# Three quarters of a down projection as seven block products: a hybrid trunk layer on one core

## The chip, the core and the metric

The kernel runs on one core of a Trainium2 chip. The core has five engines that run side by side: PE (TensorE, the matmuls), DVE (VectorE), ACT (ScalarE), POOL (GpSimd) and SP (SyncE, which issues loads). POOL and ACT issue transfers too; all go over the core's 16 DMA engines. The metric is the time of one execution on the device in microseconds (us), and less is better.

## The reference, cut to what matters

One layer: a token mixer, then the part that the change touches, a squared-ReLU MLP on 1024 frames of 1024 channels with a hidden width of 4096, and a last norm.

```
u2 = rms_norm(x, ln2) * (1.0 + scale2) + shift2
hid = jnp.square(jax.nn.relu(u2 @ w_up))      # 1024 -> 4096
x = x + gate2 * (hid @ w_down)                # 4096 -> 1024
return rms_norm(x, final_norm)
```

All is fp32.

## The kernel before

Activations lie transposed, channels on the 128 partitions and frames along the row, in tiles of 1024 frames or halves of 512. A matmul takes a 128x128 piece of a weight and 512 frames and sums into one of four banks ("mm"). To keep fp32 accuracy with the faster fp32r matmul, each operand is split: the high part is a rounding copy (ACT, whi or the first half of a hid tile), the low part what is left (DVE, wlo). A product is then three matmuls: high by high, high by low, low by high. Weight tiles (whi, wlo) have four buffers each, raw weights (wraw) three.

*Up projection.* The first four hidden tiles are plain products. The other 28 are computed in pairs by strassen_pair (L136): the weights of two column tiles, in two halves of the 1024 input channels, and the input in two halves of channels and two of frames make a 2x2 by 2x2 block product. It needs seven block products instead of eight, each of 12 matmuls (4 k x 3), with sums of weight blocks made on DVE (s12, s34), ready sums of input blocks (X), and sums of results on DVE (cu, cq, cy). up_evac squares the ReLU on ACT into hid, and POOL stores the tile to hid_d in device memory.

*Down projection* (L868). The 4096 hidden channels go in 8 blocks b of four tiles. For each, four tiles come back from hid_d through hr (POOL's queue, two buffers) and are split, hida or hid. Then for each of 8 output tiles f the plain product proj runs: 4 k x 3 x 2 halves = 24 matmuls into two banks, and DVE adds the result times gate2 into the residual y (in the code x1, loaded on SP at b = 0). The last block goes in three parts of frames (PARTS), so that the last norm overlaps with it. The first two tiles of every other block (hida) lie in the pool of hr, which exists during the up projection; the others lie in memory that the up projection's operands hold until its end.

A scheduler puts the instructions of each engine in order when the program is built; at run time each engine works strictly in that order, and each instruction waits for the data and the buffers it needs.

Of the kernel before, what the change touches and what calls it, by code (L numbers as in the profile page):

```python
# [7 lines left out]
F32 = mybir.dt.float32  # L8
# [29 lines left out]
def hybrid_trunk(tc, xT, par, hrows, crow, wada1, wada2, win, wdt, wco, wso, wo, wup, wdn, out):  # L38
# [42 lines left out]
    hid_d = dp.tile([32, P, T], F32, name="hid_d")  # L81
# [54 lines left out]
    def strassen_pair(tp_, w0, w1, X, evac):  # L136
# [29 lines left out]
        cu, cq, cy = [tp_.tile([P, H], F32, name=n) for n in ("cu", "cq", "cy")]  # L166
# [11 lines left out]
        prod(c, w34, 1, X["22"], False, True)  # L178
        tt(cy, c, cu, ALU.add)
# [638 lines left out]
    ws = [load_w(wup[i]) for i in range(4)]  # L818
# [21 lines left out]
    ph = tc.alloc_tile_pool(name="hids", bufs=2, side="right", reuse_waits="tile")  # L840
    pe_ = tc.alloc_tile_pool(name="up", bufs=2, side="right", reuse_waits="tile")
    def load_hid(i):
        hr = ph.tile([P, T], F32, name="hr")
        pool.dma_start(hr, hid_d[i])
        return hr

    for f in range(4, 32, 2):
        hid = [pe_.tile([P, T], F32, name="hid", bufs=3) for _ in (0, 1)]

        def up_evac(i, h, src):  # L850
            r = hid[i][:, hs[h]]
            act.activation(r, src, AF.Relu)
            act.activation(r, r, AF.Square)

        strassen_pair(pe_, wup[f], wup[f + 1], X, up_evac)
        for i in (0, 1):
            st_ = pool.dma_start(hid_d[f + i], hid[i])
        if f == 24:
            with tc.issue_after(st_.ins):
                hrs = [load_hid(i) for i in range(2)]  # L860
# [4 lines left out]
    p7 = tc.alloc_tile_pool(name="p7", bufs=2, reuse_waits="tile")  # L865
    xp = tc.alloc_tile_pool(name="x2", bufs=1, reuse_waits="tile")
    x1 = [[xp.tile([P, H], F32, name=f"y{f}{h}") for h in (0, 1)] for f in range(8)]
    for b in range(8):  # L868
        hid = []
        for i in range(4):  # L870
            hr = hrs.pop(0) if hrs else load_hid(4 * b + i)
            if i < 2 and b % 2 == 0:
                t = ph.tile([P, 2, T], F32R, name="hida")
            else:
                t = p7.tile([P, 2, T], F32R, name="hid", bufs=6)
            split(t[:, 0, :], t[:, 1, :], hr)
            hid.append(t)
        hh = [[t[:, 0, hs[0]], t[:, 0, hs[1]]] for t in hid]
# [103 lines left out]
```

## Time and profile before

| | before |
|---|---|
| time, median of 3 runs (lowest to highest) | 2155.35 us (2151.59 to 2156.64) |
| the profiled execution, its own time | 2155.5 us |
| span of its instructions | 2153.7 us |
| busy: PE, DVE, ACT, POOL | 98%, 65%, 40%, 5% |
| up projection's pairs | about 1520 to 1786 us |
| down projection with the last norm | 1786 to 2154 us |

The span is the time from the first to the last instruction in the trace; the time of an execution has a little around it. A busy share is a mean over the span; what an engine costs is read stage by stage.

### The profile page before, as it was taken

The numbers are of one execution on the slowest core, as the hardware profiler recorded it, in microseconds if no ns is written. First come the engines' busy times: TensorE is split into PE (matmuls) and PEld (weight loads), VectorE is DVE, ScalarE is ACT, GpSimd is POOL, SyncE is SP. The second block draws the span as 40 slices with busy tenths as digits, with TensorE's granted clock in tenths as the row PEclk, the third lists the DMA queues.
The fourth block names the chain that finished last, engine by engine and source line by source line (L and its number), as shares of the span: only waits on it lengthen the run. The fifth ranks groups of instructions, "written<-read, shape, count | busy, mean of one in ns | idle before, by whom it ended". The sixth has DMA issues, their size and how long they took to land.

```text
span 2153.7 us, 26047 instructions
## 1 busy us (share of the span) xinstructions
PE 2119.8 (98%) x9920; PEld 1731.3 (80%) x9920; DVE 1399.0 (65%) x2144; ACT 870.0 (40%) x1436; POOL 109.0 (5%) x200
## 2 busy tenths in 40 slices
PE   7999999999999999999999999999999999999998
PEld 4778878888888788888878888888888888888887
DVE  7876787765786767666885658756755555444444
ACT  4433333224565636455663321334544453211212
POOL 0000000000000000000000000021000000000003
PEclk8999999999999999999999999999999999999999
DMA  8226554123233223233356676532233346322212
GB/s 299 77 99 204 198 176 166 64 76 125 52 101 115 82 95 101 74 109 87 100 164 248 232 256 214 195 132 93 101 106 116 117 147 231 120 88 89 89 40 79
DMA packets 115472, 283.27 MB, mean 132 GB/s; under 512 B 10466, under 2 KB 45666, under 8 KB 115347
## 3 DMA queue, kind: packets, MB, share of 16 engines
q1 hardware_dynamic: 86882, 187.02, 27.0%
q0 software_dynamic: 16192, 58.73, 7.9%
q10 hardware_dynamic: 12272, 35.85, 4.2%
q8 instruction: 78, 1.28, 0.2%
q14 instruction: 48, 0.39, 0.1%
HBM read 218.45 MB, written 63.11 MB: 131 GB/s over the span
## 4 chain that ended last, share of the span: by engine, by line
PE 87%; issue 6%; DVE 3%; DMA 2%; ACT 1%; POOL 1%; SPq 0%; DVEq 0%; POOLq 0%; ACTq 0%
PE mm L145 21%; PE mm L111 19%; PE mm L114 19%; PE mm L112 19%; PE B L600 2%; PE B L605 2%; PE C L622 1%; DMA wv<-in_wada 1%; DVE wada L291 1%; PE A L577 1%; DMA x<-in_xT 1%; POOL wv L415 1%; DVE ul L46 1%; DVE x L46 0%; PE A L578 0%
## 5 line engine op out<-in xcount | busy, mean ns | idle before, releaser
L111 PE MATMUL mm<-uh,whi 128*128 128x512 f32 x768 | 303.0, 398 | 3.7 <-ACT uh L104 3.2
L112 PE MATMUL mm<-ul,whi 128*128 128x512 f32 x768 | 304.7, 397 | 0.0
L94 ACT CAST whi<-wraw 128x1024 fp32r<-128x1024 f32 x125 | 131.4, 1051 | 425.8 <-PE mm L112 403.7
L145 PE MATMUL mm<-t,whi 128*128 128x512 f32 x944 | 290.5, 390 | 2.8 <-DVE cq L43 2.8
L114 PE MATMUL mm<-uh,wlo 128*128 128x512 f32 x768 | 246.6, 396 | 1.9 <-DVE wlo L43 1.9
L43 DVE TENSOR_TENSOR wlo<-wraw,whi 128x1024 fp32r<-128x1024 f32 (+1 forms) x191 | 215.8, 1131 | 40.6 <-ACT whi L94 34.5
L145 PEld LDWEIGHTS mm<-t,whi 128*128 128x128 f32 x944 | 176.9, 188 | 40.8 <-DVE cq L43 4.3
L46 DVE SCALAR_TENSOR_TENSOR y<-mm,mcol,y 128x512 f32<-128x512 f32 (+1 forms) x136 | 92.5, 716 | 157.5 <-PE mm L114 157.4
L145 PE MATMUL mm<-t,wlo 128*128 128x512 f32 x472 | 183.0, 389 | 0.0
L111 PEld LDWEIGHTS mm<-uh,whi 128*128 128x128 f32 x768 | 144.7, 189 | 35.4 <-ACT uh L104 4.7
L114 PEld LDWEIGHTS mm<-uh,wlo 128*128 128x128 f32 x768 | 144.8, 189 | 32.1 <-DVE wlo L43 2.3
L112 PEld LDWEIGHTS mm<-ul,whi 128*128 128x128 f32 x768 | 145.0, 189 | 29.4 <-issue 0.9
L112 PE MATMUL mm<-hid,whi 128*128 128x512 f32 (+1 forms) x416 | 154.9, 374 | 0.0
L111 PE MATMUL mm<-hid,whi 128*128 128x512 f32 (+1 forms) x416 | 153.9, 373 | 0.0
L111 PE MATMUL mm<-ys,whi 128*128 128x512 f32 x384 | 148.7, 397 | 0.1
L112 PE MATMUL mm<-ys,whi 128*128 128x512 f32 x384 | 148.6, 395 | 0.0
L46 DVE SCALAR_TENSOR_TENSOR cacc<-raw,hw,cacc 128x1024 f32<-128x1024 f32 x96 | 122.9, 1281 | 27.8 <-ACT cacc L552 27.4
L145 PE MATMUL mm<-s,whi 128*128 128x512 f32 x448 | 137.9, 389 | 0.7 <-ACT cu L168 0.7
L114 PE MATMUL mm<-hid,wlo 128*128 128x512 f32 (+1 forms) x416 | 130.0, 373 | 0.0
L594 ACT ACTIVATE seg<-acb,acum 128x128 f32<-128x128 f32 x256 | 81.9, 392 | 99.6 <-PE B L600 89.7
L114 PE MATMUL mm<-ys,wlo 128*128 128x512 f32 x384 | 121.9, 392 | 0.0
L43 DVE TENSOR_TENSOR wlo<-s,whi 128x1024 fp32r<-128x1024 f32 x66 | 80.5, 1222 | 52.8 <-ACT whi L150 52.7
(272 smaller groups left out, 3968.8 us busy)
## 6 DMA issues: line engine op xcount, KB each, us to landing
wraw<-in_win SPq DMA_DIRECT2D x87, 512.0 KB, 3.6
wv<-in_wada POOLq DMA_DIRECT2D x32, 512.0 KB, 3.8
acb<-ac_d SPq DMA_DIRECT2D x64, 256.0 KB, 4.6
wraw<-in_wup SPq DMA_DIRECT2D x32, 512.0 KB, 3.4
hr<-hid_d POOLq DMA_DIRECT2D x32, 512.0 KB, 4.7
wraw<-in_wdn SPq DMA_DIRECT2D x32, 512.0 KB, 3.5
hid_d<-hid POOLq DMA_DIRECT2D x28, 512.0 KB, 4.4
gt<-gl_d SPq DMA_DIRECT2D x24, 512.0 KB, 4.6
```

The source lines that it names most:

```text
L43: return eng.tensor_tensor(out=o, in0=a, in1=b, op=op)
L46: return dve.scalar_tensor_tensor(out=o, in0=a, scalar=s, in1=b, op0=op0, op1=op1)
L94: act.copy(hi, raw)
L111: pe.matmul(o, lhsT=wh, rhs=h_, start=start, stop=False)
L112: pe.matmul(o, lhsT=wh, rhs=l_, start=False, stop=False)
L114: last_mm[0] = pe.matmul(o, lhsT=wl, rhs=h_, start=False, stop=stop)
L145: last_mm[0] = pe.matmul(o, lhsT=l_[:, s_], rhs=r_, start=first and k == j == 0, stop=k == 3 and j == 2, skip_group_check=True)
L291: return dve.tensor_tensor_reduce(out=w_, in0=w_, in1=cb, scale=0.5, scalar=prm[:, BADA + o:BADA + o + 1], op0=ALU.mult, op1=ALU.add, accu ...
L415: pool.dma_start(w_, wada2[i])
L594: act.activation(seg[:, r, :], acb[:, r, :], AF.Relu, bias=acum[:, c, hd:hd + 1], scale=-1.0)
L600: pe.matmul(Bk[o:o + 64, P * (r // 2):P * (r // 2) + P], lhsT=xd[:, r, :], rhs=seg[:, r, :], start=True, stop=True, skip_group_check=True)
L605: pe.matmul(Bk[:, 256 + P * q:256 + P * q + P], lhsT=state[:, 2 * q:2 * q + 2, :].rearrange("p r k -> p (r k)"), rhs=cf[:, cs], start=True ...
```

## The change

The hidden tiles 0 to 23 are handled as three thirds s of eight tiles (1024 hidden channels). Within a third, the hidden matrix is cut in two halves of channels and two of frames, and the down weights in two halves of input channels and pairs p of output tiles: again a 2x2 by 2x2 block product with seven products.

- *Up projection:* the pairs are now tiles (8s + k, 8s + k + 4), so that one pair holds all four blocks of hidden tile k of a third. It writes one tile hp of seven blocks: up_evac fills four, DVE makes the other operands with four subtractions (one in place), and one store takes all seven to op_d. The tiles 24 to 27 take the place of 0 to 3 in the plain part; 28 to 31 are two pairs without block operands.
- *strassen_pair* here takes keep=False: cy uses the buffer of cq, not one of its own.
- *Down projection:* hid_block(0) (tiles 24 to 27) as plain products first, then per third seven products n, each over all four pairs p before the next n, then hid_block(1) (tiles 28 to 31) in PARTS. The operand of a product (four k tiles of 512 frames) is loaded from op_d in two transfers through hr (now three buffers) and split into an op tile (five buffers). Weight blocks come raw (dr, four buffers, SP) from a re-tiled copy of the weights; products 2 to 5 need sums on DVE (s12, s34). The low part for products 2 to 5 is made by DVE as before; for 0, 1 and 6 ACT writes the negated high part and a load that adds to what is there (accum_op, on POOL's queue) adds the raw weights.
- One bank per pair is kept over two products (0 and 1, 3 and 4, 5 and 6); product 2 has its own. After a product, DVE (for the first also ACT) reads the bank into the residual y or into a running sum per pair, cus (c0 to c3), which is folded into y at the end.

```diff
+    def stage(src):
+        hr = ph.tile([P, 2, H], F32, name="hr")
+        pool.dma_start(hr, src)
+        return hr
...
+    ups = [(8 * s + k, 8 * s + k + 4, s, k) for s in range(3) for k in range(4)] + [(28, 29, 3, 4), (30, 31, 3, 6)]
+    for i0, i1, s, k in ups:
+        hp = pe_.tile([P, 7, H], F32, name="hp")
...
+        strassen_pair(pe_, wup[i0], wup[i1], X, up_evac, keep=False)
...
+        x11, x12, x21, x22, t1, t2, t4 = [hp[:, i, :] for i in range(7)]
+        tt(t1, x12, x11, ALU.subtract)
+        tt(x12, x22, x12, ALU.subtract)
+        tt(t2, x22, t1, ALU.subtract)
+        tt(t4, x21, t2, ALU.subtract)
+        st_ = pool.dma_start(op_d[s, k], hp)
...
+    op = tc.alloc_tile_pool(name="ops", bufs=5, reuse_waits="tile")
...
+    def operand(srcs):
+        t = op.tile([P, 2, 4, H], F32R, name="op")
+        for q, s_ in enumerate(srcs):
+            split(t[:, 0, 2 * q:2 * q + 2, :], t[:, 1, 2 * q:2 * q + 2, :], s_())
+        return t
...
+    def gate(f, h, src):
+        stt(x1[f][h], src, mcol[:, 40 + f:41 + f], x1[f][h], ALU.mult, ALU.add)
+
+    hh, hl = hid_block(0)
...
+    for s in range(3):
+        bank, s12 = [None] * 4, [None] * 4
+
+        def piece(n, p):
+            f0, f1 = 2 * p, 2 * p + 1
+            if n < 2:
+                return raw_of(s, [(f0, n)])[0], wdt_[s, f0, :, hs[n]]
...
+            if n == 2:
+                a21, a22 = raw_of(s, [(f1, 0), (f1, 1)])
+                a11, = raw_of(s, [(f0, 0)])
+                s12[p] = ds.tile([P, 2, H], F32, name="s12")
+                tt(s12[p][:, 0, :], a21, a22, ALU.add)
+                tt(s12[p][:, 1, :], s12[p][:, 0, :], a11, ALU.subtract)
+                return s12[p][:, 1, :], None
...
+        for n, blk in enumerate((0, 2, 5, 4, 3, 1, 6)):
+            t = operand([lambda q=q: stage(op_d[s, 2 * q:2 * q + 2, :, blk, :].rearrange("k p t -> p k t")) for q in (0, 1)])
+            first = n in (0, 2, 3, 5)
+            for q in (0, 1):
+                wh = wp.tile([P, T], F32R, name="whi")
+                wl = wp.tile([P, T], F32R, name="wlo")
+                for i in (0, 1):
+                    val, src = piece(n, 2 * q + i)
+                    act.copy(wh[:, hs[i]], val)
+                    if src is None:
+                        tt(wl[:, hs[i]], val, wh[:, hs[i]].bitcast(F32), ALU.subtract)
+                    else:
+                        act.mul(wl[:, hs[i]], val, -1.0)
+                        pool.dma_start(wl[:, hs[i]], src, accum_op=ALU.add)
+                for i in (0, 1):
+                    p = 2 * q + i
+                    if first:
+                        bank[p] = mm.tile([P, H], F32, name="mm")
+                    o = bank[p]
+                    for k in range(4):
+                        c_ = slice(i * H + k * P, i * H + k * P + P)
+                        for j, (l_, r_) in enumerate(((wh, 0), (wh, 1), (wl, 0))):
+                            pe.matmul(o, lhsT=l_[:, c_], rhs=t[:, r_, k, :], start=first and k == j == 0,
+                                      stop=k == 3 and j == 2, skip_group_check=True)
+                    if n == 0 and s == 0:
+                        act.copy(cus[p], o)
+                    elif n in (0, 2):
+                        tt(cus[p], o, cus[p], ALU.add)
+                    else:
+                        gate(2 * p + (n in (3, 5, 6)), int(n in (3, 4, 5)), o)
...
+    hh, hl = hid_block(1)
+    ws = [load_w(wdn[1, i]) for i in range(4)]
```

How this moves instructions is seen in the order of the built programs. ACT at the start of the down projection, before: hida are the first two split tiles, 26 rows ahead of the others, and the whi casts (L94) are those of the first down weights; hid_14121 and hid_14122 are the last results of the up projection.

```order
L150 CAST whi_13996<-wraw_13992 128x1024
L100 CAST hida_14281<-hr_13847 128x1024
L100 CAST hida_14284<-hr_13849 128x1024
...
L94 CAST whi_14431<-wraw_14429 128x1024
L852 ACTIVATE hid_14121<-cy_14155 128x512
L853 ACTIVATE hid_14121<-hid_14121 128x512
L94 CAST whi_14497<-wraw_14495 128x1024
L100 CAST hid_14289<-hr_14287 128x1024
L100 CAST hid_14294<-hr_14292 128x1024
L852 ACTIVATE hid_14122<-cu_14153 128x512
L853 ACTIVATE hid_14122<-hid_14122 128x512
```

The same place after (L95 is the cast of the fourth weight tile, op_14297 and op_14302 are the four tiles of hid_block(0), op_14575 is the first block operand, hp_14132 the last up result).

```order
L95 CAST whi_14511<-wraw_14509 128x1024
L101 CAST op_14297<-hr_13859 128x1024
L101 CAST op_14297<-hr_13861 128x1024
L101 CAST op_14302<-hr_14303 128x1024
L859 ACTIVATE hp_14132<-cu_14163 128x512
L860 ACTIVATE hp_14132<-hp_14132 128x512
L101 CAST op_14302<-hr_14307 128x1024
L101 CAST op_14575<-hr_14576 128x1024
```

What was done in two places, a pair ahead and behind the fourth weight cast, is now all behind that cast.

DVE there, before: the low part of the fourth weight tile, the second two splits, then the sums of f0 and f1 (y00 to y11) leave their banks.

```order
L43 TENSOR_TENSOR wlo_14499<-wraw_14495,whi_14497 128x1024
L43 TENSOR_TENSOR hid_14289<-hr_14287,hid_14289 128x1024
L43 TENSOR_TENSOR hid_14294<-hr_14292,hid_14294 128x1024
L46 SCALAR_TENSOR_TENSOR y00_14265<-mm_14305,mcol_74,y00_14265 128x512
L46 SCALAR_TENSOR_TENSOR y01_14266<-mm_14306,mcol_74,y01_14266 128x512
L46 SCALAR_TENSOR_TENSOR y10_14267<-mm_14335,mcol_74,y10_14267 128x512
L46 SCALAR_TENSOR_TENSOR y11_14268<-mm_14336,mcol_74,y11_14268 128x512
```

After, from the low part of the same weight tile on:

```order
L43 TENSOR_TENSOR wlo_14513<-wraw_14509,whi_14511 128x1024
L43 TENSOR_TENSOR op_14297<-hr_13859,op_14297 128x1024
L43 TENSOR_TENSOR op_14297<-hr_13861,op_14297 128x1024
L43 TENSOR_TENSOR op_14302<-hr_14303,op_14302 128x1024
L43 TENSOR_TENSOR op_14302<-hr_14307,op_14302 128x1024
L43 TENSOR_TENSOR op_14575<-hr_14576,op_14575 128x1024
L46 SCALAR_TENSOR_TENSOR y00_14277<-mm_14319,mcol_74,y00_14277 128x512
L43 TENSOR_TENSOR op_14575<-hr_14580,op_14575 128x1024
L46 SCALAR_TENSOR_TENSOR y01_14278<-mm_14320,mcol_74,y01_14278 128x512
L43 TENSOR_TENSOR op_14664<-hr_14665,op_14664 128x1024
L46 SCALAR_TENSOR_TENSOR y10_14279<-mm_14349,mcol_74,y10_14279 128x512
```

Four splits of hid_block(0) now stand there, and three half operands of the third (op_14575, op_14664) stand between the first evacuations.

POOL's queue in the second third, after: hr are operand loads, wlo the loads that add the raw weights for product 6 of the first third (wlo_15131, wlo_15169) and product 0 of the second (wlo_15216, wlo_15256).

```order
L847 DMA hr_15490<-op_d_93 128x2x512
L960 DMA wlo_15131<-in_wdt_ 128x512 x2
L960 DMA wlo_15169<-in_wdt_ 128x512 x2
L847 DMA hr_15494<-op_d_93 128x2x512
L847 DMA hr_15567<-op_d_93 128x2x512
L960 DMA wlo_15216<-in_wdt_ 128x512 x2
L960 DMA wlo_15256<-in_wdt_ 128x512 x2
L847 DMA hr_15571<-op_d_93 128x2x512
L847 DMA hr_15656<-op_d_93 128x2x512
```

Before, this queue held only the loads of hr here; now the adding loads stand behind operand loads that wait for a free hr buffer.

## Rows read from the trace of the kernel before

**Rows 1.** The page of the profile: the span, the busy time of each engine with its share, and of the 40 slices of the span PE's busy tenths, the granted clock and the DMA share.
```profile
span 2153.7 us, 26047 instructions
PE 2119.8 (98%) x9920; PEld 1731.3 (80%) x9920; DVE 1399.0 (65%) x2144; ACT 870.0 (40%) x1436; POOL 109.0 (5%) x200
PE   7999999999999999999999999999999999999998
PEclk8999999999999999999999999999999999999999
DMA  8226554123233223233356676532233346322212
```

**Rows 2.** Busy time by stretch (pairs of the up projection, start of the down projection, a later block of it, its end). Columns: stretch, length, then busy us and instructions of PE, PE's weight loads, DVE, ACT and POOL, the granted clock, the DMA share and GB/s.
```profile
1530.00:1660.00 130.00, 130.00 (x575) 107.66 (x574) 69.30 (x90) 62.86 (x90) 7.48 (x14) 1.00 0.33 114
1790.00:1834.00 44.00, 44.00 (x196) 36.38 (x195) 24.03 (x28) 11.38 (x11) 4.25 (x8) 1.00 0.72 256
1834.00:1878.00 44.00, 44.00 (x196) 36.45 (x195) 20.68 (x25) 8.46 (x9) 2.32 (x5) 1.00 0.32 98
2098.00:2153.70 55.70, 45.09 (x309) 41.26 (x307) 27.43 (x73) 15.97 (x34) 21.66 (x24) 0.92 0.22 76
```

**Rows 3.** The waits of PE from 1520 us to the end: who waited for whom, us in total, times, longest.
```profile
PE st L233 <- DVE sdg L43: 4.0, 1, 4.0
PE mm L145 <- ACT cu L168: 0.7, 1, 0.7
```

**Rows 4.** Busy time in one long stretch of each kind of matmul: the pairs of the up projection and the plain blocks of the down projection (columns as in rows 2).
```profile
1540.00:1780.00 240.00, 240.00 (x1061) 198.72 (x1060) 126.72 (x163) 116.87 (x165) 16.01 (x30) 1.00 0.36 123
1800.00:2090.00 290.00, 290.00 (x1281) 240.23 (x1280) 136.99 (x160) 55.53 (x53) 13.80 (x26) 1.00 0.32 101
```

**Rows 5.** PE in order of time at the first matmuls of the down projection: start, duration, engine, line, operation, count (a matmul's 0.39 us overlap the next one's start).
```profile
1785.83 0.39 PE L112 MATMUL mm<-hida,whi 128*128 128x512 f32 x1
1786.06 0.39 PE L111 MATMUL mm<-hida,whi 128*128 128x512 f32 x1
1786.28 0.39 PE L112 MATMUL mm<-hida,whi 128*128 128x512 f32 x1
1786.51 0.62 PE L114 MATMUL mm<-hida,wlo 128*128 128x512 f32 x2
1786.96 0.39 PE L111 MATMUL mm<-hida,whi 128*128 128x512 f32 x1
```

**Rows 6.** ACT in order of time around the same place, with the idle time before an instruction and what ended it.
```profile
1785.58 1.06 ACT L94 CAST whi<-wraw 128x1024 fp32r<-128x1024 f32 x1 [0.47 <-PE mm L145]
1786.54 2.00 ACT L100 CAST hid<-hr 128x1024 fp32r<-128x1024 f32 x2
1796.23 1.05 ACT L94 CAST whi<-wraw 128x1024 fp32r<-128x1024 f32 x1 [6.50 <-PE mm L112]
1797.19 1.04 ACT L100 CAST hid<-hr 128x1024 fp32r<-128x1024 f32 x1
1799.75 1.06 ACT L100 CAST hid<-hr 128x1024 fp32r<-128x1024 f32 x1 [1.52 <-DMA hr<-hid_d]
```

**Rows 7.** DVE there, and the loads of y on SP's queue (start, the time over which they were issued, count).
```profile
1786.66 1.23 DVE L43 TENSOR_TENSOR wlo<-wraw,whi 128x1024 fp32r<-128x1024 f32 x1 [0.17 <-ACT whi L94]
1787.81 2.35 DVE L43 TENSOR_TENSOR hid<-hr,hid 128x1024 fp32r<-128x1024 f32 x2
1785.58 14.63 SPq L886 DMA_DIRECT2D y<-x_d  x16
```

**Rows 8.** Transfers: two of POOL's load issues (from the timeline), the time from issue to landing of all 32 loads of hr (min/median/max), the stores of 256 KB in the stage before (KB each, median us to landing), and the busiest stretch of the DMA engines near the place (columns as in rows 2).
```profile
1789.32 0.54 POOL L844 DMA_DIRECT2D hr<-hid_d  x1 [3.39 <-DVE hid L43]
1790.54 0.54 POOL L844 DMA_DIRECT2D hr<-hid_d  x1
DMA to landing us min/median/max: 3.7/4.7/9.2
hid_d<-hid POOLq DMA_DIRECT2D x8, 256.0 KB, 2.3
1786.00:1798.00 12.00, 12.00 (x54) 9.86 (x54) 6.44 (x8) 5.46 (x7) 1.59 (x3) 1.00 0.93 358
```

**Rows 9.** Instructions of DVE and ACT from 1520 to 2100 us by line, operation and shape: count, busy us and mean ns of one, idle time before them and what ended it.
```profile
L46 DVE SCALAR_TENSOR_TENSOR y<-mm,mcol,y 128x512 f32<-128x512 f32 x115 | 81.2, 747 | 140.3 <-PE mm L114 140.3
L43 DVE TENSOR_TENSOR hid<-hr,hid 128x1024 fp32r<-128x1024 f32 x24 | 29.3, 1224 | 18.5 <-ACT hid L100 18.1
L43 DVE TENSOR_TENSOR cu<-mm,cu 128x512 f32<-128x512 f32 x28 | 19.3, 691 | 42.4 <-PE mm L145 42.4
L43 DVE TENSOR_TENSOR s<-wraw 128x512 f32<-128x512 f32 x26 | 17.9, 688 | 0.4
L43 DVE TENSOR_TENSOR wlo<-wraw,whi 128x512 fp32r<-128x512 f32 x14 | 9.6, 685 | 0.0
L100 ACT CAST hid<-hr 128x1024 fp32r<-128x1024 f32 x24 | 25.1, 1052 | 41.5 <-DMA hr<-hid_d 20.7 <-PE mm L114 19.5 <-DVE hid L43 1.3
L150 ACT CAST whi<-wraw 128x512 fp32r<-128x512 f32 x14 | 8.7, 623 | 6.3 <-PE mm L145 6.3
L853 ACT ACTIVATE hid<-hid 128x512 f32<-128x512 f32 x56 | 35.3, 633 | 1.7
```

More of the change, by code (lines that the diff above doesn't have):

```diff
@@ L178, in strassen_pair @@
         prod(c, w34, 1, X["22"], False, True)
+        cy = tp_.tile([P, H], F32, name="cy") if keep else cq
         tt(cy, c, cu, ALU.add)
@@ L912, in hybrid_trunk, with hid_block @@
-    for p_ in (pst, xp, p7, ph, rp, cp2, mm, dp, wp, cp):
+    cus = [xp.tile([P, H], F32, name=f"c{p}") for p in range(4)]
+    def operand(srcs):
[3 more added lines that the diff above has]
+        return t
+    def hid_block(b):
+        hh, hl = [], []
+        for j in (0, 1):
+            t = operand([lambda i=4 * b + 2 * j + q: hrs.pop(0) if hrs else stage_hid(i) for q in (0, 1)])
+            for q in (0, 1):
+                hh.append([t[:, 0, 2 * q + h, :] for h in (0, 1)])
+                hl.append([t[:, 1, 2 * q + h, :] for h in (0, 1)])
+        return hh, hl
@@ new lines, in gate, with raw_of @@
+    def gate(f, h, src):
+        stt(x1[f][h], src, mcol[:, 40 + f:41 + f], x1[f][h], ALU.mult, ALU.add)
+    hh, hl = hid_block(0)
+    for f in range(8):
+        if f % 2 == 0:
+            w = load_w(wdn[0, f // 2])
+        for h in (0, 1):
+            sp.dma_start(x1[f][h], x1_d[f, :, hs[h]])
+        ps = proj(w, hh, hl, nk=4, base=(f % 2) * 512)
+        for h in (0, 1):
+            gate(f, h, ps[h])
+    def raw_of(s, parts):
+        r = ds.tile([P, 2, H], F32, name="dr")
+        for i, (f, k) in enumerate(parts):
+            sp.dma_start(r[:, i, :], wdt_[s, f, :, hs[k]])
+        return [r[:, i, :] for i in range(len(parts))]
@@ new lines, in hybrid_trunk @@
+    for p in range(4):
+        for f, h in ((2 * p, 1), (2 * p + 1, 1), (2 * p + 1, 0)):
+            gate(f, h, cus[p])
+    ds.release()
+    p7 = tc.alloc_tile_pool(name="p7", bufs=2, side="right", reuse_waits="tile")
+    hh, hl = hid_block(1)
+    ws = [load_w(wdn[1, i]) for i in range(4)]
+    for t0, tw, onpool in PARTS:
+        h, o = t0 // H, t0 % H
+        win_ = slice(o, o + tw)
+        st = Stats(p7, pst, pool, 6, width=tw)
+        xs_ = [x1[f][h][:, win_] for f in range(8)]
+        for f in range(8):
+            ps, = proj(ws[f // 2], [[v[h][:, win_]] for v in hh], [[v[h][:, win_]] for v in hl],
+                       nk=4, base=(f % 2) * 512, halves=(0,), width=tw)
+            stt(xs_[f], ps, mcol[:, 40 + f:41 + f], xs_[f], ALU.mult, ALU.add)
+            st.add(xs_[f])
+            if f in onpool:
+                act.mul(xs_[f], xs_[f], prm[:, FNORM + f:FNORM + f + 1])
+        rbs_ = p7.tile([P, H], F32, name="ut")[:, :tw]
+        act.copy(rbs_, st.rb)
+        for f in range(8):
+            if f in onpool:
+                tt(xs_[f], xs_[f], rbs_, ALU.mult, eng=pool)
+            else:
+                stt(xs_[f], xs_[f], prm[:, FNORM + f:FNORM + f + 1], st.rb, ALU.mult, ALU.mult)
+            (sp if f % 2 else act).dma_start(out[f, :, t0:t0 + tw], xs_[f])
@@ L970 @@
         "wup": tiles(a["w_up"][0]),
-        "wdn": kblocks(a["w_down"][0]),
+        "wdt_": np.stack([tiles(a["w_down"][0][1024 * i:1024 * i + 1024]) for i in range(3)]),
+        "wdn": kblocks(a["w_down"][0][3072:]),
     }
```

90 lines of the change are left out of this document (30 added, 60 removed).

## The prediction

> **What bounds the kernel now.** I read the page's table of engines and its slices first [rows 1]: TensorE (PE) is busy for 98% of the span at full granted clock, and only the first and the last slices fall short. The table by stage comes next [rows 2]: in the up and in the down projection PE is busy for all of each window while VectorE (DVE) has about half its time free, ScalarE (ACT) more, and the DMA engines two thirds. The waits of PE from 1520 us to the end [rows 3] come to 4.7 us, 4.0 of them in the tail. So both projections run at the pace of the matmuls, and time is saved or lost as matmuls, or as gaps between them.
>
> **The matmuls removed.** Before, the down projection is 8 blocks x 8 column tiles x 4 k x 2 halves x 3 = 1536 matmuls of 512 columns (the last block's in narrower pieces, no less work). After, two blocks stay (2 x 192) and three thirds of 7 products x 4 pairs x 4 k x 3 = 336 each replace six: 1392. That is 144 fewer. The pace is the same for both kinds: 240 us hold 1061 matmuls of the pair stage, 290 us hold 1281 of the plain one [rows 4], 0.2262 and 0.2264 us each (a window counts those at its edges too, and the first five matmuls of [rows 5] take 1.13 us, so 0.2265). **144 x 0.2265 = 32.6 us off the path.**
>
> **Up stage, at nothing.** Each of 12 pairs gets four more 128x512 subtractions on DVE, about 0.69 us each by the like ones of the weights [rows 9], 2.8 us a pair. A pair is 84 matmuls, 19.0 us, and DVE is busy for 126.7 of 240 us there [rows 4], 53%; 67% after. A store of 1.8 MB takes the place of two of 0.5 MB, 41 GB/s more on 123 [rows 4]. hp has two buffers, so a store has a whole pair to drain. With cy in cq's slots, two slots still serve sums that ACT empties in the next microseconds. The cover is PE's 19.0 us; without it the stage would lose 12 x 2.8 = 33 us.
>
> **The start of the down projection, 6.6 us.** Before, PE goes from the last pair to the first down matmul at 1785.83 without a gap [rows 5], because two of the four operand tiles (hida) were split a pair earlier in memory of their own; the other two are split behind ACT's cast of the fourth weight tile, at 1786.54 [rows 6]. After, all four lie in the new pool, and the order shown puts their casts behind that weight cast, which itself waits for PE's last up product (1785.58, [rows 6]).
> - The first cast ends at 1787.6, so PE starts 1.8 us late. After four matmuls (0.9 us) it needs the low part; DVE's first split ends at 1787.81 + 1.22 = 1789.0 [rows 7]: 0.5 us more.
> - The fourth tile's load needs a buffer that this first split frees, so POOL issues it at 1789.1. Such loads land in 3.7 to 9.2 us [rows 8]; before, those issued at 1789.32 and 1790.54 were used at 1797.2 and 1799.75 [rows 6, 8], while the 16 loads of y went out on SP. I take 6.5, near the first of these: cast and split end 2.3 us after landing, at 1797.9, against 1796.3 where PE reaches the tile's high part (32 matmuls on) and 1797.6 for the low part: 0.7 us in all. The bounds are 0 and 3.
> - f0 and f1 fill all four sum banks. On DVE the evacuation of y00 now stands behind the split of the first block operand's first half. Its load leaves when the second split ends (1790.2); before, the load issued then took 9.2 us [rows 8]. With that: landed 1799.4, split 1801.7, y00 emptied 1802.4, and f2, which PE could begin at 1799.7, waits 2.7 us for the bank. y01 stands behind the second half, some 3.5 us later on the same queue: 0.9 us more. The bounds are 0 and 6.
>
> Sum 1.8 + 0.5 + 0.7 + 2.7 + 0.9 = **6.6 us**, from 2.3 (loads at 3.7 us) to about 12.
>
> **The block stage, at nothing, if its feeders keep up.** An operand is 48 matmuls, 10.9 us; a third 76.1 us.
> - DVE, with [rows 9]: two splits 2.4, four evacuations 2.8 to 3.0, and for products three to six four low parts 2.7, plus eight sums 5.5 for the third and four 2.8 for the fifth and sixth. The cheap three cost 5.3, the others about 13.5, 8.1, 10.8 and 10.8: 59 of 76.1 us, but 43 of 43.5 in that run of four. The cover is a lead: four weight tiles of two pairs let weights be two operands ahead, five operand buffers operands four ahead, and an emptied bank is needed again only after three pairs, 8.2 us.
> - ACT: two casts 2.1, four weight casts 2.5 and where it also negates 2.5 more: 7.1 of 10.9.
> - DMA: 36 weight loads and 12 accumulating ones of 256 KB and 14 operand loads of 512 KB, 19.9 MB in 76.1 us, 262 GB/s. The busiest stretch, 1786 to 1798, moves 358 at a share of 0.93 [rows 8], much of it in 2 KB rows (y) as here.
> - The accumulating loads have no row. From below: a plain 256 KB transfer, 2.3 us from issue to landing [rows 8] and 0.7 us of the engines at 358 GB/s. From above: I cannot bound it by a row; three passes over the bytes instead of one make 2.2 us of the engines. A low tile is free three tiles (16.3 us) before PE needs it; ACT takes 2.5, so two accumulates have 13.8 us. Twelve come in a row of six tiles (seventh product, then the next third's first two), so stalls begin when one after the other they cost (13.8 + 5 x 5.44)/12 = 3.4 us each. I take the 0.7 to 2.2, as nearest to the plain rows: no stall. With three passes the DMA rate would be 345 GB/s, still under 358/0.93 = 385.
>
> The Trainium skill bears on this: Collectives: The Full Stack, section The bandwidth ceiling, says that the adder in the DMA path costs nothing itself, but that an add needs two source reads and so runs at half the copy's rate. By that an accumulate would take 1.4 us of the engines here, an estimate from that page, and the sum would stay as it is; no run here shows it yet.
>
> **The end.** The last block's operands and its first weight tiles come from slots freed operands earlier, and the tail is as before; the twelve folds of the sums, 9 us of DVE, lie in the seventh product's and its neighbour's spare time. Nothing.
>
> **Sum.** The profiled execution took 2155.5 us, the median of the timed runs is 2155.35, so no correction is due. 2155.5 - 32.6 + 6.6 = **2129.5 us**.
>
> **Rivals.**
> - The start is hidden: the loads land at 3.7 us, or the matmuls are ordered around them. 2122.9 to 2125.2. Against it, ACT's casts wait for PE's own last product. 0.10.
> - DVE or the weights fall behind in part: were products three to six to run 10% over their 43.5 us, or an accumulate to cost 3.7 us, each third would lose about 4 us: 2142, and up to 2151. For it: 43 of 43.5 us and in-order waits on ACT; against it, the lead. 0.14.
> - Slower: the accumulates serialise at a low rate on POOL's queue. At 3.4 us each nothing is lost, at 4.2 each third loses 9 us and the gain is gone, at 5 it loses 12 x 5 - 41 = 19 us: 2186. For it: no row shows their speed, and operand loads stand before them in one queue. Against: it is six times the plain transfer's engine time. 0.11.
> - The 62 transfers of a third run as if alone, 48 x 2.3 + 14 x 4.7 = 176 us against 76: 2430 us. Against: 16 of y (4.2 MB) went out in 14.6 us beside other loads [rows 7, 8], 0.9 us each. 0.02. Beside it stands the rule of the Trainium skill, DMA: Bandwidth & Descriptors, section Bandwidth, to batch transfers to 1 MiB or more for three quarters of the peak: here 256 KB loads overlap to 358 GB/s, so the trace does not bear it out for many in flight.
> - Smaller losses that end within 0.2% of before: 0.05.
>
> **How the numbers follow.** My forecast, 2125 to 2136, has 0.58. With the hidden start (0.10) and most of the second rival (0.12 of 0.14) the range 2122 to 2147 holds 0.8; the accumulates, bounded by no row, are what lies above. Faster by over 0.2% (4.3 us, about what a measurement can tell from no change): 0.58 + 0.10 + 0.14 = 0.82. Within: 0.05. Slower: 0.13.
>
> **What would show it.** 144 fewer matmuls at the same pace; PE gaps of 1 to 3 us within 20 us of the first down matmul, ended by ACT's cast of op, DVE's split of op and DVE's y; no PE wait on the accumulating DMA (wlo from in_wdt_), which would land in 2 to 6 us; DVE near full in products three to six and slack after. The prediction is wrong if PE waits over 5 us in a third, for a low part from the DMA or for a bank, or if the start costs over 12 us.

## The result and the profile after

The changed kernel takes 2132.31 us (median of 4 runs, 2131.68 to 2134.14) against 2155.38 us before on the same chip: a ratio of 0.9897, 95% interval 0.988 to 0.9914. That is 23.1 us less, where 26 were forecast (2129.5 us, range 2122 to 2147). The execution profiled below took 2131.68 us. One execution of the later run after_again took 3507.24 us at a mean granted clock of 0.555 and is left out of that run's median.

The head of its page, which answers [rows 1]: engines with busy time, share and instructions, then the clock granted to PE and the DMA share in 40 slices.

```profile
span 2129.9 us, 26252 instructions
PE 2090.5 (98%) x9776; PEld 1705.4 (80%) x9776; DVE 1474.1 (69%) x2278; ACT 928.4 (44%) x1554; POOL 152.1 (7%) x242
PEclk8999999999999999999999999999999999999998
DMA  8126554123133223232347586453144446988922
```

9776 matmuls are 144 fewer than before; PE is still what the kernel waits for. New are the four slices of the DMA row with 6, 9, 8, 8 tenths, from about 1810 to 2023 us, where [rows 1] have 3, 4, 6, 3.

The table by stage, against [rows 2, 4]: the up projection, the start of the down projection (two rows), the thirds (three rows), the rest. After PE, PEld, DVE, ACT and POOL stand the granted clock, the DMA share and GB/s.

```profile
1540.00:1780.00 240.00, 240.00 (x1060) 198.79 (x1060) 152.87 (x209) 114.56 (x164) 9.08 (x17) 1.00 0.43 160
1786.00:1800.00 14.00, 12.77 (x46) 9.51 (x47) 5.79 (x6) 5.96 (x7) 3.27 (x5) 0.88 0.94 347
1800.00:1840.00 40.00, 37.72 (x164) 30.20 (x164) 21.82 (x27) 17.35 (x25) 12.20 (x16) 1.00 0.95 292
1840.00:1916.00 76.00, 76.00 (x337) 62.94 (x336) 50.76 (x68) 37.59 (x58) 21.32 (x27) 1.00 0.89 264
1916.00:1992.00 76.00, 76.00 (x337) 62.94 (x336) 54.40 (x74) 35.43 (x55) 20.68 (x27) 1.00 0.89 263
1992.00:2068.00 76.00, 76.00 (x337) 62.91 (x336) 63.70 (x87) 26.21 (x37) 8.29 (x12) 1.00 0.57 169
2068.00:2130.00 62.00, 51.18 (x329) 46.56 (x327) 28.45 (x75) 18.14 (x36) 21.84 (x24) 0.91 0.20 68
```

PE is busy for all of the up projection and of the thirds; time is lost at the start of the down projection and at a lower clock in the last row. The chain that ended last (start, length, what) has the same two unbroken stretches, the last pairs and the three thirds:

```profile
1520.87 263.93 PE mm L146 x1163
1836.51 228.48 PE mm L969 x1008
```

The kernel before has the first of them too:

```profile
1521.63 264.14 PE mm L145 x1164
```

The pairs run as long as before, and 1008 matmuls in 228.48 us are 0.2267 each. Between the two lie 192 plain matmuls, 43.5 us at 0.2265, so 264.1 + 43.5 = 307.6 us would separate their starts if nothing were lost; they are 315.6 apart. **The start costs 8.0 us**, where 6.6 were forecast. PE's rows with a wait in it (start, length, idle time ahead and its releaser):

```profile
1786.86 1.68 PE L112 MATMUL mm<-op,whi 128*128 128x512 f32 x4 [1.85 <-ACT op L101]
1797.29 1.19 PE L112 MATMUL mm<-op,whi 128*128 128x512 f32 x4 [0.30 <-ACT op L101]
1801.91 0.50 PE L112 MATMUL mm<-op,whi 128*128 128x512 f32 x1 [1.24 <-DVE y L46]
1805.79 0.50 PE L112 MATMUL mm<-op,whi 128*128 128x512 f32 x1 [0.87 <-DVE y L46]
1808.97 0.50 PE L112 MATMUL mm<-op,whi 128*128 128x512 f32 x1 [0.17 <-DVE y L46]
```

These are the waits of the forecast, in its order: the first cast, the fourth tile, the banks of y. They sum to 4.4 us. The windows of one us behind the first wait show what it did not have (columns as above):

```profile
1787.00:1788.00 1.00, 1.00 (x4) 0.68 (x4) 1.00 (x2) 1.00 (x2) 0.00 (x0) 0.68 0.92 360
1788.00:1789.00 1.00, 1.00 (x4) 0.59 (x3) 1.00 (x2) 1.00 (x2) 0.45 (x1) 0.50 1.02 418
1789.00:1790.00 1.00, 1.00 (x4) 0.81 (x3) 1.00 (x2) 0.87 (x2) 0.40 (x2) 0.50 1.01 369
1790.00:1791.00 1.00, 1.00 (x4) 0.77 (x4) 0.53 (x1) 0.00 (x0) 1.00 (x3) 0.61 0.88 309
1791.00:1792.00 1.00, 1.00 (x6) 0.83 (x5) 0.00 (x0) 0.00 (x0) 0.69 (x1) 1.00 0.83 285
```

The granted clock falls to 0.50, the lower of the two levels, behind the idle 1.85 us, and PE's first 12 matmuls, from 1786.86 to 1791.4, take 4.5 us instead of 2.7: 1.8 us, the wait for the low part hidden in them. 4.4 + 1.8 = 6.2; each wait also costs about 0.16 us that its idle time does not show, since a matmul of 0.39 us overlaps the next at 0.2265 and not across a wait, 0.8 us for five. Of the remaining 1 us some 0.4 is in the first matmul behind each of the four later waits, which takes about 0.11 us longer (0.50 in place of 0.39 in the last three rows); the rest has no row.

From the end of the thirds (1836.51 + 228.48 = 2065.0) to the end of the span are 64.9 us, against 63.4 before: in 2090 to 2096 us the granted clock is 0.72, where before it was 1.00 in that place. The whole: -32.6 + 8.0 + 1.5, and the pairs' start 0.8 us earlier (1520.87 against 1521.63) is -23.9, the spans differ by 23.8.

### The profile page after: what moved, and what is told of

It reads as the page before. It is cut to its first block, busy times and chain, and to the rows that moved or that the text cites. A ratio compares the mean times of both kernels' runs of the same rounds, so it can differ in the third digit from the quotient of the medians.

```text
span 2129.9 us, 26252 instructions
## 1 busy us (share of the span) xinstructions
PE 2090.5 (98%) x9776; PEld 1705.4 (80%) x9776; DVE 1474.1 (69%) x2278; ACT 928.4 (44%) x1554; POOL 152.1 (7%) x242
## 4 chain that ended last, share of the span: by engine, by line
PE 78%; issue 14%; DVE 4%; DMA 3%; ACT 1%; POOL 1%; SPq 0%; DVEq 0%; POOLq 0%; ACTq 0%
PE mm L146 20%; PE mm L112 13%; PE mm L115 13%; PE mm L113 13%; PE mm L969 11%; PE B L602 1%; PE B L607 1%; DMA wv<-in_wada 1%; PE C L624 1%; DMA y<-x_d 1%; DVE wada L293 1%; POOL wv L417 1%; PE A L579 1%; DVE ul L46 1%; DVE x L46 0%
## 5 line engine op out<-in xcount | busy, mean ns | idle before, releaser
L95 ACT CAST whi<-wraw 128x1024 fp32r<-128x1024 f32 x101 | 106.0, 1050 | 261.4 <-PE mm L113 206.5
L43 DVE TENSOR_TENSOR wlo<-wraw,whi 128x1024 fp32r<-128x1024 f32 (+1 forms) x167 | 186.4, 1117 | 40.2 <-ACT whi L95 34.1
L969 PE MATMUL mm<-op,whi 128*128 128x512 f32 x672 | 207.0, 389 | 0.0
L43 DVE TENSOR_TENSOR wlo<-s,whi 128x1024 fp32r<-128x1024 f32 (+1 forms) x114 | 111.9, 994 | 54.5 <-ACT whi L151 53.6
L969 PEld LDWEIGHTS mm<-op,whi 128*128 128x128 f32 x672 | 126.1, 188 | 26.3
L969 PE MATMUL mm<-op,wlo 128*128 128x512 f32 x336 | 130.7, 389 | 0.0
L46 DVE SCALAR_TENSOR_TENSOR y<-mm,mcol,y 128x512 f32<-128x512 f32 (+1 forms) x100 | 69.6, 705 | 76.8 <-PE mm L969 41.4
```

What stands on the lines that cost most here:

```text
L43: return eng.tensor_tensor(out=o, in0=a, in1=b, op=op)
L46: return dve.scalar_tensor_tensor(out=o, in0=a, scalar=s, in1=b, op0=op0, op1=op1)
L95: act.copy(hi, raw)
L969: pe.matmul(o, lhsT=l_[:, c_], rhs=t[:, r_, k, :], start=first and k == j == 0, stop=k == 3 and j == 2, skip_group_check=True)
```

## The experiments

Four jobs beside the first; in each the kernel before ran too (medians 2156.7, 2155.9, 2157.6 and 2157.5 us). The columns "start", "thirds" and "rest" are read from the profiled execution of each as above: what is lost between the last pairs and the thirds over 307.6 us, the length of the three thirds from the first to the last of their matmuls (228.5 without a wait), and what is left to the end of the span.

| version | median us | ratio to before, 95% | start | thirds | rest |
|---|---|---|---|---|---|
| changed kernel | 2132.31 | 0.988 to 0.9914 | 8.0 | 228.5 | 64.9 |
| acc_plain | 2132.46 | 0.9867 to 0.9906 | 7.4 | 228.5 | 63.4 |
| acc_twice | 2172.57 | 1.0043 to 1.0088 | 8.2 | 272.4 | 63.1 |
| late_w | 2130.40 | 0.9856 to 0.9894 | 5.7 | 229.8 | 66.4 |
| gates_first | 2130.13 | 0.9854 to 0.9890 | 4.6 | 231.0 | 63.5 |
| acc_dve | 2129.92 | 0.9858 to 0.9890 | 7.6 | 228.5 | 63.1 |
| both | 2128.26 | 0.9856 to 0.9886 | 3.1 | 228.9 | 63.3 |
| one_third | 2152.85 | 0.9982 to 1.0001 | 8.4 | 76.2 (one) | |
| after_again | 2132.84 | 0.9877 to 0.9907 | | | |
| both_dve | 2124.69 | 0.9829 to 0.9870 | 3.1 | 228.5 | 63.1 |
| acc_dve_2 | 2131.85 | 0.9868 to 0.9906 | 8.5 | 228.5 | 66.1 |
| after_ctl (changed kernel) | 2132.17 | 0.9870 to 0.9909 | 7.6 | 232.9 | 63.4 |
| both_dr8 | 2138.38 | 0.9891 to 0.9923 | 3.0 | 240.8 | 63.4 |

**The accumulating loads as plain loads, and twice.** My theory: they are hidden. Rival: they bound the block stage.

```diff
-                        pool.dma_start(wl[:, hs[i]], src, accum_op=ALU.add)
+                        pool.dma_start(wl[:, hs[i]], src)
```

> The loads that add the raw weights to the negated high part become plain loads of the raw weights (the low part is then wrong by the high part; all else is computed). Theory, PE sets the pace of the thirds and the adding loads are hidden: 2131 to 2133 us, PE still without a wait inside the thirds, and the DMA share of the first two thirds falls from 0.89 to about 0.78 (an adding load seems to take 1.5 us of the 16 engines, a plain one 0.78; 12 x 0.72 us of 76). Rival, the adding loads slow the feeding of PE: 2120 to 2128 us.

```diff
                         pool.dma_start(wl[:, hs[i]], src, accum_op=ALU.add)
+                        pool.dma_start(wl[:, hs[i]], src, accum_op=ALU.add)
```

> Each adding load is issued twice in a row onto the same bytes (the low part is then wrong by the raw weights). Theory, what hides them is DMA time, and little of it is left: the share of a third goes from 0.89 by 12 x 1.5 / 76 = 0.24 to more than 1, so the first two thirds become bound by the transfers, about 86 instead of 76 us each, less the lead: 2142 to 2157 us, with PE waiting for wlo from the DMA. Rival, only the latency of one load counts and the lead of two operands covers two of them: 2131 to 2134 us.

As plain loads they leave the time as it was, so what the addition costs was hidden; the DMA share of the first two thirds is 0.81 to 0.84, where 0.78 was expected. Twice they make the kernel slower than before by 0.65%: 2172.57 us, above both forecasts. Waits that the change does not show (us in total, times, longest) are there, of PE on the low parts and of POOL's second load on its first:

```profile
PE mm L970 <- DMA wlo<-in_wdt_: 27.4, 7, 7.2
POOL wlo L961 <- DMA wlo<-in_wdt_: 64.8, 26, 7.7
```

The thirds lose 44 us, 27.4 in PE's seven waits and most of the rest at the lower clock behind them (0.89 from 1914 to 1990 us, 0.91 from 1990 to 2064). But it does not show a limit by DMA time, as the theory had it: the DMA share from 1914 to 1990 us is 0.85. The second load onto the same bytes is issued only when the first has landed, and on POOL's queue the operand loads stand behind it. So the doubling adds a round trip to POOL's queue that the changed kernel does not have, and how much time the accumulates have to spare there stays open.

**The two orders at the start.** One puts the cast and the split of the fourth weight tile behind the four operand splits, on ACT and on DVE (sa and sd are the last cast and the last subtraction of hid_block(0)). The other puts DVE's subtractions of the first two block operands behind the last evacuation of f1 (g1); ACT's casts of them start as before, at 1799.01 and 1802.87 us against 1798.89 and 1802.76.

```diff
         if f % 2 == 0:
-            w = load_w(wdn[0, f // 2])
+            with tc.issue_after(sa.ins) if f == 6 else contextlib.nullcontext():
+                with tc.issue_after(sd.ins) if f == 6 else contextlib.nullcontext():
+                    w = load_w(wdn[0, f // 2])
```

> The cast and the split of the fourth down weight are ordered behind the four operand splits of hid_block(0), on ACT and on DVE; nothing else is changed. Theory, PE's first wait (2.0 us) and the low clock behind it come from that cast: the first wait shrinks to about 0.5 us, the granted clock stays at 1.0, and 2 to 3.5 us go: 2129 to 2130.5 us. Rival, the wait comes back at the first evacuations, since on SP the loads of y stand behind a raw weight load that needs this split: PE waits 2 us or more for y or the banks instead, 2131 to 2134 us.

```diff
         for n, blk in enumerate((0, 2, 5, 4, 3, 1, 6)):
-            t = operand([lambda q=q: stage(op_d[s, 2 * q:2 * q + 2, :, blk, :].rearrange("k p t -> p k t")) for q in (0, 1)])
+            with tc.issue_after(g1.ins) if s == 0 and n < 2 else contextlib.nullcontext():
+                t = operand([lambda q=q: stage(op_d[s, 2 * q:2 * q + 2, :, blk, :].rearrange("k p t -> p k t")) for q in (0, 1)])
```

> On DVE and ACT, the splits of the first two block operands are ordered behind the evacuation of f1 (y11); nothing else is changed. Theory, PE's bank waits (1.24, 0.87 and 0.17 us) come from splits that wait for loads while they stand ahead of the evacuations: those waits go, 2129.5 to 2131 us, and the thirds start as much earlier. Rival, y itself lands late or the chain of operand loads, now later, makes the first third wait: 2132 to 2136 us.

> Both orders of the earlier two runs at once: ScalarE's cast and VectorE's split of the fourth down weight tile stand behind the four operand splits of the first block, and the splits of the first two block operands stand behind the last evacuation of f1. Alone the first took the wait ahead of the first down matmul from 1.85 to 0.33 us and left 2.1 us of waits on banks; the second took the waits on banks away and left the 1.86 us. If the two waits are independent, as the account of the start has it (the first belongs to ScalarE's order, the banks to VectorE's), both go: 2.5 to 4 us under the changed kernel, 2127 to 2130 us, and a PE without a wait of over 0.7 us from the last up product to the thirds. Rival (one pays for the other: the later weight cast or the later operand splits turn up as waits at f6 or in the first third): 2130 to 2133 us, with new waits of 2 us or more on op, whi or y.

In late_w the first wait falls from 1.85 to 0.33 us, and the waits on banks stay (of three, the first is shown; PE's rows as above):

```profile
1784.46 1.20 PE L114 MATMUL mm<-op,whi 128*128 128x512 f32 x4 [0.33 <-ACT op L103]
...
1798.40 0.50 PE L114 MATMUL mm<-op,whi 128*128 128x512 f32 x1 [0.82 <-DVE y L46]
```

In gates_first the waits on banks are gone up to 1836 us and the first stays:

```profile
1788.00 1.19 PE L112 MATMUL mm<-op,whi 128*128 128x512 f32 x4 [1.86 <-ACT op L101]
1789.45 0.76 PE L113 MATMUL mm<-op,whi 128*128 128x512 f32 x2 [0.26 <-DVE op L43]
```

In `both`, three waits are left before the thirds; the third is for the high part of the fourth tile:

```profile
1784.62 1.20 PE L114 MATMUL mm<-op,whi 128*128 128x512 f32 x4 [0.33 <-ACT op L103]
1786.20 0.73 PE L115 MATMUL mm<-op,whi 128*128 128x512 f32 x2 [0.38 <-DVE op L43]
...
1794.81 1.19 PE L114 MATMUL mm<-op,whi 128*128 128x512 f32 x4 [1.07 <-ACT op L103]
```

And the clock goes with the first wait. From 1780 to 1800 us the granted clock is 0.91 in seven of the eight profiles with a wait of 1.85 us there (acc_plain has 1.00), and 1.00 in all four with 0.33. The first row is of gates_first, the second, in the next fence, of late_w (columns as in the table by stage):

```profile
1780.00:1800.00 20.00, 17.89 (x71) 13.78 (x70) 9.69 (x9) 11.53 (x15) 3.44 (x6) 0.91 0.77 261
```

```profile
1780.00:1800.00 20.00, 17.80 (x74) 13.12 (x73) 10.98 (x11) 10.78 (x14) 4.50 (x7) 1.00 0.85 308
```

The losses 8.0, 5.7, 4.6 and 3.1 show two causes, the order of the weight tile ahead of the first matmul and DVE's order ahead of the banks, as the forecast's first and third points had them. They are not quite independent: alone they give back 2.3 and 3.4 us, together 4.9. What is paid back is the fourth tile, the forecast's second point: 0.30 us of wait in the changed kernel, 0.62 in late_w, 1.07 in `both`, where no wait over 0.7 was expected. There its load, issued when the first split has freed a buffer, lands only at 1793.7 us, and the first matmul starts 2.2 us earlier than in the changed kernel. On time, `both` is in its first theory's band, as late_w and gates_first are in theirs, but the three ratios overlap: the profiles tell these versions apart, the times hardly. gates_first loses another 2.5 us in its second and last thirds, taken up below.

**One third alone.** The other two thirds' tiles are stored plain and multiplied in four plain blocks.

```diff
-    for s in range(3):
+    for s in range(1):
         bank, s12 = [None] * 4, [None] * 4
...
+    for b in range(2, 6):
+        hh, hl = hid_block(b, hid2_d)
+        for f in range(8):
...
+            ps = proj(w, hh, hl, nk=4, base=(f % 2) * 512)
```

> The change for one third of the blocks alone: one quarter of the down projection as block products, the other two thirds' hidden tiles stored plain by the up pairs and multiplied in four plain blocks, with the start, the pools and the end as in the changed kernel. 48 matmuls fewer than before instead of 144. Theory (each third takes 48 x 0.2265 = 10.9 us off, and all of the loss is at the start and in the tail, paid once): 2155.4 - 10.9 + 7 to 9.5 = 2151.5 to 2154 us, 0.1 to 0.2% under the kernel before, and 21.8 us over the changed one. Rival (the loss comes with each third, by the feeders or the folds of the sums): the fixed loss would be a third of 9, and the time 2147.5 to 2149 us.

2152.85 us lies in the first theory's band and outside the rival's: each third gives its 10.9 us, and the loss of 8.4 us stands at the start, paid once. One third alone would hardly be worth it (3.1 us, its interval just reaches no change); three are.

**DVE's own low parts, and the changed kernel again.**

```diff
-                    if src is None:
+                    if True:
                         tt(wl[:, hs[i]], val, wh[:, hs[i]].bitcast(F32), ALU.subtract)
```

> The changed kernel with one part of its block stage undone: VectorE subtracts the low part of every block weight itself, and ScalarE's negation and the accumulating load are gone. In each third 12 accumulating loads (some 1.5 us of the 16 engines each, an estimate from the plain and the doubled accumulates) leave the queues, and VectorE takes 12 subtractions of 0.68 us more in the three cheap products, 8.2 us a third. Theory (the accumulates are hidden, and so is VectorE in the three products where it has most time free): same as the changed kernel, 2130 to 2134 us, no wait of PE inside the thirds, a DMA share in the thirds 0.1 to 0.2 under the 0.89 of the changed kernel, VectorE at about 59 to 62 of 76 us. Rival (VectorE is nearly full, so the accumulates are what makes the block stage fit): 4 us or more a third, 2142 us or more, with waits of PE on VectorE's wlo.

> The changed kernel once more, beside the others on the same chip: 2131 to 2134 us. Its second profile tells which of the small losses of the first come in each execution: the wait of 1.85 us ahead of the first down matmul and the waits on the banks should return within 0.3 us; the low granted clock just behind the first wait and in the last block may come or not.

> The version with VectorE's own low parts again, beside the changed kernel on the same chip and with more rounds. If the accumulates are hidden, the two differ by less than 1 us (both 2130 to 2133) and the 0.18% of the last comparison was scatter of the stages ahead of the down projection and of the clock in the last block; if they cost something, 2 us or more (2128 to 2130 against 2131 to 2134).

> The changed kernel beside the other two: 2130 to 2134 us. Its profile should show the wait of 1.85 us ahead of the first down matmul and some 2 us of waits on the banks again, 7 to 8 us lost from the last pair to the first third, and no wait inside the thirds; the low granted clock behind the first wait and in the last block may come or not.

after_again is used for its times alone. Beside it acc_dve came out 2.9 us under the changed kernel, at the lower edge of its theory's band; beside after_ctl, acc_dve_2 0.3. The intervals overlap in both comparisons, so on the median no cost of the accumulates is shown, and DVE, busy for 59 to 66 us of each third in acc_dve, has room for the 12 subtractions. But the profile of after_ctl, of an execution of 2136.25 us, is not free of waits in the thirds, where none was expected. PE's waits there:

```profile
PE mm L969 <- DVE y L46: 3.9, 2, 2.1
```

And its chain up to the first of them, with the loads between one stretch of PE and the next:

```profile
1838.17 70.51 PE mm L969 x311
...
1910.83 8.54 DMA dr<-in_wdt_
...
1920.56 4.66 DMA dr<-in_wdt_
...
1926.76 5.84 DMA dr<-in_wdt_
...
1934.66 6.53 DMA dr<-in_wdt_
...
1942.51 0.67 DVE y L46
...
1943.32 44.78 PE mm L969 x197
```

Four loads of raw weights follow one another, each waiting for the buffer that a sum on DVE frees; behind them DVE's evacuation of a bank is late, and PE waits 1.8 us. The same chain comes again in the last third, with a wait of 2.1 us at 2021.86. It is the third product, with three loads and two sums for each pair. The table of the stretch in which its loads begin, 1890 to 1930 us, in after_ctl (columns as above):

```profile
1890.00:1930.00 40.00, 40.00 (x178) 33.14 (x177) 20.35 (x27) 17.90 (x28) 14.22 (x18) 1.00 1.03 282
```

And in acc_dve_2:

```profile
1890.00:1930.00 40.00, 40.00 (x179) 33.10 (x178) 28.88 (x41) 15.19 (x21) 4.27 (x6) 1.00 0.71 235
```

With the accumulates the engines are full for these 40 us; without them they are at 0.71, and with plain loads in their place (acc_plain) at 0.91. Over the five profiles with accumulates and the stock feed (the changed kernel's two, late_w, gates_first, `both`) the thirds lose 0, 4.4, 1.3, 2.5 and 0.4 us, over the four without accumulates (acc_plain, acc_dve, acc_dve_2, both_dve) nothing. In these nine profiles the waits come only with the accumulates. That full engines are the reason is likely, but they are not enough by themselves: the changed kernel's first profile has 1.04 and 295 GB/s in the same stretch and no wait.

**The best version, and a remedy that failed.** both_dve has the two orders and DVE's low parts. both_dr8 has the two orders, keeps the accumulates and gives the raw weights eight buffers of one half in place of four of two.

> The two orders at the start together with VectorE's own low parts in place of the accumulating loads. Theory (the accumulates are hidden; what is left to lose is some 3 us at the start): within 1.5 us of the version with the two orders alone, 2127 to 2130 us, with the thirds at 228.5 to 229 us and the DMA share in them near 0.7. Rival (the accumulates cost 2 us somewhere that the profiles do not name, since the version with VectorE's low parts came out at a ratio of 0.9874 against 0.9892 for the changed kernel): 2124 to 2126.5 us. A second rival: with f1's evacuations ahead of the operand splits and more subtractions behind them, VectorE is late in the first third: 2130 us or more, with waits of PE on wlo or op there.

```diff
-        r = ds.tile([P, 2, H], F32, name="dr")
-        for i, (f, k) in enumerate(parts):
-            sp.dma_start(r[:, i, :], wdt_[s, f, :, hs[k]])
-        return [r[:, i, :] for i in range(len(parts))]
+        rs = [ds.tile([P, H], F32, name="dr", bufs=8) for _ in parts]
+        for r, (f, k) in zip(rs, parts):
+            sp.dma_start(r, wdt_[s, f, :, hs[k]])
+        return rs
```

> The version with the two orders at the start, accumulating loads kept, with one change in the third, fifth and sixth products' feed: the raw pieces of the weights lie in eight buffers of one half each instead of four of two halves, in the same memory, so that a load no longer waits for a whole pair of halves and up to eight are under way instead of four in the single ones. In the last profile of the changed kernel PE lost 3.9 us inside the thirds, at the end of a chain of four loads of raw pieces of 4.7 to 8.5 us, each waiting for the buffer that the one before it freed; without the accumulating loads the same loads land a microsecond sooner and no wait appears. Theory (the stall is that chain of round trips, and the accumulates only lengthen it): the thirds run without a wait of PE although the accumulates stay, 2123.5 to 2126 us, as the version without accumulates (2124.7). Rival (the accumulates take the DMA engines or POOL's queue themselves): waits of PE in the thirds of up to 4 us in some executions remain, 2127 to 2130 us, as the version with the two orders alone (2128.3).

both_dve takes 2124.69 us (2123.39 to 2125.07): 7.5 us under the changed kernel of the same job, each of its runs under each of that one's. It has the lowest median found, 1.5% under the kernel before. It lies in the band of its first rival (accumulates that cost 2 us unseen) and below its theory's. It came out below `both` by 3.6 us, but in another job, and the intervals of the two ratios overlap; the profile of `both` is of its fastest execution (2124.92 us) and lost 0.4 us in the thirds. That its slower ones (to 2129.81) lose more there is not shown. Nor is it explained why the low parts on DVE would gain here, and on the median nothing without the two orders.

both_dr8 takes 2138.38 us, 10 us more than `both` in another job, and the intervals of their ratios do not overlap: my theory fell, and the time lies above the rival's band too. Deeper prefetch did harm. The thirds lose 12.3 us; PE's waits there:

```profile
PE mm L977 <- ACT whi L963: 5.0, 3, 3.0
PE mm L977 <- DVE c L43: 3.0, 1, 3.0
```

In its chain stand the load of an operand and the longest of the raw weights:

```profile
1916.27 10.40 DMA hr<-op_d
...
1997.11 12.36 DMA dr<-in_wdt_
```

The landing times of the raw loads from 1894 to 1930 us, in both_dr8:

```profile
DMA to landing us min/median/max: 4.2/5.7/13.0
```

And in `both`:

```profile
DMA to landing us min/median/max: 3.3/4.4/6.1
```

From 1894 to 1930 us the DMA share is 1.03 in both_dr8 and 0.99 in `both`: with the engines this full, more loads under way made each land later, and the one that is needed next was among them. The operand loads in that stretch land later too, 7.6 us in the median against 5.8, and the accumulates 9.0 against 7.0. So waiting for a buffer is not what sets the pace of these loads; that the engines' work in that stretch does fits the rival's mechanism, and is not shown by itself.

## Why the prediction was right, and where it was off

- **Matmuls removed, -32.6 us: right.** 144 fewer, at 0.2267 us in the thirds; one_third confirms it for a single third.
- **Up stage at nothing: right.** 263.93 us against 264.14; DVE 152.9 of 240 us, 64%, where 67% was forecast, the store 160 GB/s in all against the forecast 164.
- **The start, 6.6 us forecast, 8.0 measured: the mechanism right, the size of one term off.** The first wait is 1.85 us (1.8 forecast), the fourth tile's 0.3 us, the wait on the banks 1.24 + 0.87 + 0.17 = 2.3 us (3.6 forecast; PE came later to them). The term that failed is the low part's 0.5 us: I priced what follows the first wait at the full clock, and at the granted 0.50 it took 1.8. In acc_plain, where the clock did not fall behind the same wait, the low part's wait is 0.25 us and the fourth tile's 0.96; the loss is 7.4, against 7.6 to 8.5 in the six profiles with the same orders where it fell, so on balance the low clock cost about 1 us at most. And I counted a wait as its idle time alone, without the 0.16 us of overlap lost with it.
- **The end at nothing: off by 1.5 us** in the profiled execution, with the lower clock in the last block; in eight of the ten other profiles in the table the rest takes 63.1 to 63.5 us as before, in two 66.
- **The block stage at nothing: right in the first profile, and with far less to spare than I wrote.** The step that fails is the DMA sum, 262 GB/s against 385 possible: a mean over the third. Accumulates and raw loads for the sums come together, and there the engines are full at 282 to 295 GB/s for 40 us. The accumulates land later than the 2 to 6 us forecast (the first row is POOL's issue, in ns; the second the time to landing, over the thirds of the changed kernel):

```profile
L960 POOL DMA_DIRECT2D wlo<-in_wdt_ x36: 847/942/1542, 1818.3 to 2046.0; - x36
DMA to landing us min/median/max: 3.8/7.2/11.1
```

What one costs the engines can be estimated from the shares in the first two thirds: 0.89 with accumulates, 0.81 to 0.84 with plain loads (acc_plain; the first row), 0.70 without either (acc_dve; the second row).

```profile
1914.00:1990.00 76.00, 76.00 (x337) 62.92 (x337) 54.45 (x74) 35.81 (x54) 16.53 (x26) 1.00 0.83 265
1840.00:1916.00 76.00, 76.00 (x337) 62.94 (x336) 58.98 (x82) 32.37 (x47) 9.97 (x14) 1.00 0.70 220
```

At the middle value, 0.13 x 76 / 12 = 0.8 us for a plain load, and 0.19 x 76 / 12 = 1.2 us for an accumulate, half as much again; both inside the forecast 0.7 to 2.2. Summed over their own packets in the trace, an accumulate took 1.45 us of the 16 engines in the changed kernel and the plain load in its place 0.87 in acc_plain, 1.7 times as much; the operand loads beside the accumulates took less than without them (0.76 against 0.86 us for 256 KB, changed kernel and acc_dve), so the share grows by less. The Trainium skill, Collectives: The Full Stack, section The bandwidth ceiling, has the addition at half the copy's rate, which was 1.4 us by my estimate: the trace agrees in direction, with a factor of 1.5 to 1.7 instead of 2. Of the rivals, the accumulates that serialise appear only where they are doubled and each second one waits for the first; "the weights fall behind in part" happens in some executions, by up to 4.4 us for all three thirds together instead of 4 for each.

## What to carry to other kernels

Here the saving in matmuls arrived in full, since PE was the bound, and most of what was lost stood at the seam where buffers, casts and first loads change: look there for which engine's order puts other work ahead of the first operand, and move that work behind it; two such orders gave back 5 us of 8. Check DMA capacity in the densest stretch, product by product, and not as a mean over the stage; where the engines were full, deeper prefetch made it worse. If DVE has a third of its time free, it can make the low part that a load would add up: here that cost nothing, and the thirds then ran without a wait. And a version meant to double one cost can add another: look at what the doubled instruction waits for.

## What the runs showed of the hardware

- Behind a wait of 1.85 us after long full work the clock granted to PE fell from 1.00 to 0.50 and was back at 1.00 by 1791 us, four us after the restart (the changed kernel's first profile); it fell in seven of eight profiles with such a wait, and in none of four where the wait was 0.33 us. In late_w, where the wait's idle time fell by 1.5 us, the start lost 2.3 us less; between gates_first and `both` it was 1.5 less, since the fourth tile's wait took part of the gain.
- A load that adds raised the DMA engines' share by 1.2 us for 256 KB against about 0.8 for a plain one (estimates from the shares; 1.45 against 0.87 by their own packets), and POOL took 0.94 us for its issue.
- Two adding loads onto the same bytes went one after the other: the second was issued when the first had landed, 64.8 us of POOL's waits in 26 loads (acc_twice).
- At a DMA share of 1.0, up to eight single loads under way in place of four went with a median landing of 5.7 us instead of 4.4, the longest 13.0 instead of 6.1, and thirds 11.9 us longer (both_dr8 against `both`).
